# Low parts of sixteen context weights: from VectorE subtractions to accumulating transfers and ScalarE casts

## The chip, the core and the metric

The kernel runs on one core of a Trainium2 chip. The metric is the device time of one execution in microseconds; lower is better. The time before the change is the median of three runs.

## The reference

Three blocks are computed one after another on 512 tokens of width 1024: a first block (differential attention, a multi-scale pooling branch, attention over 256 memory tokens, a gated mix, a feed-forward part with a causal convolution of width 3), and two layers of a second model that has a latent stream of 512 tokens and a context stream of 256 tokens. The part that bears on the change is the layer called even, whose input weight (`in_ev_w` on the device) and output weight (`in_ev_o`) are used for the context as well as for the latent tokens:

```python
def project(h):
    aq, ak, av, ag, bq, bk, bv, bg = split_cols(h @ w_in, EVEN_WIDTHS)
    aq = rms_norm_2(heads(aq, A_HEADS), q_gain)
    ak = rms_norm_2(heads(ak, A_KV_HEADS), k_gain)
    ...
aq, ak, av, ag, bq, bk, bv, bg = project(h_lat)
c_aq, c_ak, c_av, c_ag, c_bq, c_bk, c_bv, c_bg = project(h_ctx)
...
y_ctx = jnp.concatenate([oa_c * jax.nn.silu(c_ag), ob_c * jax.nn.silu(c_bg)], axis=-1) @ w_out
```

All inputs are float32. The first block's two residual sums, `x + rms_norm(mix @ w_out)` and `x + rms_norm(ff)`, are what runs at the two boundaries named below.

## The kernel before

Activations lie feature-major: a tile has 128 features on the partitions and 512 tokens (256 for the context) along the free axis, eight tiles for 1024 features. A weight is taken in pieces of 1024 x 128 (512 KB), and one piece gives one **product**: 128 output features for all tokens, summed over eight blocks of 128 inputs. Every large product is split in three terms. A float32 operand is divided in a high part, which is the value rounded to TensorE's own format fp32r (`whi` for a weight, `hh` for an activation), and a low part, the rest (`wlo`, `hl`); `mm3` issues high x high, high x low and low x high into the same PSUM tile, so a product is 24 matmuls. All of them are recorded at the helper `mm`, L286.

Preparing a piece of weight takes three steps, in the class `Product` (L455 and on). `load` lets SP bring the piece from HBM into a buffer `raw` (L466; three buffers). `parts` lets ScalarE cast it to `whi` (L476; three buffers) and VectorE subtract, `wlo = raw - whi` (L483; two buffers). `step` issues the matmuls of one block and, after the last, the product's evacuation. A second way of making the low part is written out in `parts` and `low`, for products whose `adds` is set: it is never taken in this kernel, because the list `adding` holds False throughout.

What runs when is decided while the program is built. Products wait in `queue`, in batches. `fetch` (L334) keeps two products ahead of TensorE loaded and one of them prepared. A batch that serves as **filler** is advanced a little at a time between the steps of other work, `advance(filler, us)`, so that TensorE has products to do while VectorE and ScalarE work on something else. Each engine then runs its own list in that order, and waits at an instruction until its inputs and buffers are ready; nothing overtakes.

Two fillers matter here:

- At the **first boundary** (the profile's 591 to 641 us) the first block's mixing part ends. `post_norm` (L1490 and on) scales the eight tiles of the w_out product (`acc`, L1495), adds them to the residual (`x`, L1496) and takes their squares (ScalarE `sqa` and `ta`, L574 and L577, VectorE sum L578); the next normalisation splits `x` in `hh` (ScalarE, L522) and `hl` (VectorE, L523). The filler is the context's keys, values and queries of the even layer: eight pieces of `in_ev_w`.
- At the **second boundary** (1067 to 1115 us) the first block ends. `post_norm` does the same with the w_down product, and the even layer's latent input is normalised and modulated behind it (`mod_scale`: VectorE `ta` L1049, ScalarE `hh` L1051, VectorE `hl` L1052). The filler is the context's output projection `ctx_out`: eight pieces of `in_ev_o`, each evacuated into the context's residual (`cx`, L1069) and sent to HBM.

Before each filler TensorE does the last products of w_out and w_down; behind the first come the up-projection's pieces (`in_w_up`), behind the second those of `in_ev_w` for the latent tokens. Both take the plain way. SP's queue holds, beside the loads, the copies of `x` and `cx` to HBM (`xd`, `cxd`). GpSimd's work in this kernel is the division by the softmax sums (L974, L1193) and a few small tiles.

Of the kernel before, what the change touches and what calls it, by code (L numbers as in the profile page):

```python
# [21 lines left out]
KD = 8  # L22
# [179 lines left out]
def body(nc, tc, A, out, dbg=None):  # L202
# [16 lines left out]
    wp = pool(top, "wp")  # L219
# [88 lines left out]

    queue, ahead, adding = deque(), [], [False]
    END = object()
    current = [None, 0]

# [18 lines left out]

    def fetch():  # L334

        while len(ahead) < (3 if adding[0] else 2) and queue:
            pull()
        for p in ahead[:2 if adding[0] else 1]:
            p.parts()
        if ahead:  # L340
            ahead[0].low()
# [43 lines left out]
    def lazy(weights, n, products):  # L385

        made = []

        def bind(p, i):
            if not made:  # L390
                made.extend(products())
            p.x, p.evac = made[i].x, made[i].evac

        for i, src in enumerate(weights):
            p = Product(src, None, None, n, src.shape[-1] // P)
            p.bind = lambda p=p, i=i: bind(p, i)
            yield p

    def when(ready, products):
# [51 lines left out]
    class Product:  # L451
# [8 lines left out]
        adds = False  # L460

        def load(self):
            self.adds = adding[0] and not self.same and self.keep[0] is wp
            if not self.same:
                self.raw = tl(wp, [P, 1024], "raw", NRAW)
                nc.sync.dma_start(out=self.raw[:, :self.kt * P], in_=self.src)  # L466
# [37 lines left out]
    def product(src, x, evac, n=T, kt=KD):  # L504
        return [Product(src, x, evac, n, kt)]
# [885 lines left out]

    ec = Even(hc, None, ep, kpc, vtc)
    cmix = pair(cmp_, "m", n=C)
    filler = Batch(chain(ec.keys_values(True), ec.queries(0), ec.queries(1)))

    ff = {}

# [143 lines left out]
    def ctx_out(m):  # L1541
        def evac(ps):
            residual(cx[m], 0, 1, ps, m)
            nc.sync.dma_start(out=cxd[m], in_=cx[m])
        return product(A["ev_o"][m], cmix, evac, C)

    filler = Batch(p for m in range(KD) for p in ctx_out(m))
    firsts = Batch(lazy([A["ev_w"][ct] for ct in (4, 5, 0, 1, 2, 3)], T, lambda: chain(el.queries(0), el.keys_values())))
    advance(filler, 2.5)
    ss = post_norm(y, fss.rms_now(filler), "norm_ffn_post", filler)  # L1550
# [55 lines left out]
    def lat_items(n):  # L1606
# [3 lines left out]
    filler = Batch(chain(el.queries(1), lat_gate(0), lat_gate(1), when(lambda: 3 in el.qd, el.queries(2)), lat_gate(2),  # L1610
                         when(lambda: 7 in el.qd, el.queries(3)), *(lat_gate(m) for m in range(3, 8))))
# [269 lines left out]
```

## Time and profile before

| | |
|---|---|
| median of three runs | 1740.97 us (1740.2 to 1741.71) |
| the profiled execution's own time | 1742.39 us |
| its span, first to last instruction | 1740.4 us |
| mean granted TensorE clock | 0.982 |
| TensorE, VectorE, ScalarE, GpSimd busy | 95%, 75%, 50%, 11% of the span |
| DMA | 227.06 MB, 130 GB/s mean |

All times of instructions are from the profiled execution, in microseconds from the start of its span. Busy time is the sum of the instructions' durations on an engine; idle time before a group is put down to what ended it. A chain of waits is followed backwards from an end: at each step to what released it. The granted clock is the share of full speed that the chip gave TensorE in a stretch.

### The profile page before, as it was taken

How to read it: one execution, taken by the hardware profiler on the slowest of the kernel's cores; microseconds unless marked ns; L12 is line 12 of the kernel's file. 1: busy time of each engine (PE TensorE's matmuls, PEld its weight loads, DVE VectorE, ACT ScalarE, POOL GpSimd, SP SyncE). 2: the span in 40 equal slices, each digit the busy share in tenths (PEclk: the TensorE clock that was granted, in tenths of full speed). 3: DMA queues.
4: the chain of work that ended last, by engine and by line, in shares of the span. 5: the costliest groups of instructions: out<-in, count | busy, mean ns of one | idle time of the engine just before them, and what ended most of it. 6: DMA issues, size and time to landing. Idle time of an engine off the chain costs nothing.

```text
span 1740.4 us, 24824 instructions
## 1 busy us (share of the span) xinstructions
PE 1659.9 (95%) x8712; PEld 1392.3 (80%) x8712; DVE 1303.5 (75%) x2605; ACT 876.6 (50%) x1628; POOL 191.3 (11%) x261
## 2 busy tenths in 40 slices
PE   8999999999999989999999999899999999999897
PEld 6878878888787878888887778777888787888677
DVE  7967776777599587755775687678887665999984
ACT  6542225555333446654774343346677544554462
POOL 0120000000000000001000000002233101233200
PEclk9999999999899989999999999999999899999999
DMA  5345556445175343433332554442222446444131
GB/s 198 121 140 181 182 179 161 121 111 144 65 254 182 123 139 98 127 100 127 108 109 85 195 183 159 153 121 74 61 74 73 134 140 187 130 119 115 62 122 59
DMA packets 84875, 227.06 MB, mean 130 GB/s; under 512 B 12048, under 2 KB 24720, under 8 KB 84752
## 3 DMA queue, kind: packets, MB, share of 16 engines
q1 hardware_dynamic: 81728, 219.46, 40.5%
q10 hardware_dynamic: 3024, 6.03, 1.0%
q8 instruction: 69, 1.13, 0.3%
q14 instruction: 54, 0.44, 0.1%
HBM read 181.93 MB, written 9.44 MB: 110 GB/s over the span
## 4 chain that ended last, share of the span: by engine, by line
PE 75%; DVE 16%; ACT 3%; DMA 3%; issue 2%; POOL 0%; SPq 0%; DVEq 0%; ACTq 0%; POOLq 0%
PE mm L286 62%; PE tr L286 6%; PE s L286 3%; DVE mixf L1789 3%; PE tr L612 3%; DVE wlo L483 2%; DVE ptl L519 2%; ACT sb L1188 1%; DVE sb L1183 1%; DVE mj L863 1%; DMA cb<-in_cond 1%; DVE x L1496 1%; DVE hl L519 1%; ACT whi L476 0%; DVE acc L1495 0%
## 5 line engine op out<-in xcount | busy, mean ns | idle before, releaser
L286 PE MATMUL mm<-hh,whi 128*128 128x512 f32 (+1 forms) x1472 | 583.9, 397 | 18.2 <-ACT whi L476 7.0
L286 PE MATMUL mm<-hh,wlo 128*128 128x512 f32 (+1 forms) x1472 | 564.2, 383 | 8.9 <-DVE wlo L483 8.9
L286 PE MATMUL mm<-hl,whi 128*128 128x512 f32 (+1 forms) x1472 | 563.5, 383 | 2.0 <-DVE hl L1052 1.9
L476 ACT CAST whi<-raw 128x1024 fp32r<-128x1024 f32 (+2 forms) x264 | 268.6, 1018 | 336.1 <-PE mm L286 257.4
L483 DVE TENSOR_TENSOR wlo<-raw,whi 128x1024 fp32r<-128x1024 f32 (+2 forms) x264 | 311.7, 1181 | 85.5 <-PE mm L286 68.8
L286 PEld LDWEIGHTS mm<-hh,wlo 128*128 128x128 f32 x1472 | 281.5, 191 | 68.8 <-DVE wlo L483 12.5
L286 PEld LDWEIGHTS mm<-hh,whi 128*128 128x128 f32 x1472 | 282.7, 192 | 64.2 <-ACT whi L476 8.4
L286 PEld LDWEIGHTS mm<-hl,whi 128*128 128x128 f32 x1472 | 283.1, 192 | 45.8 <-DVE hl L1052 3.1
L1193 POOL TENSOR_SCALAR sb<-sb,l 128x256 f32<-128x256 f32 (+3 forms) x128 | 125.5, 981 | 919.2 <-DVE l L1192 859.1
L518 ACT CAST pth<-tr 128x512 fp32r<-128x512 f32 (+2 forms) x240 | 101.3, 435 | 91.7 <-PE tr L612 90.5
L519 DVE TENSOR_TENSOR ptl<-tr,pth 128x512 fp32r<-128x512 f32 (+2 forms) x240 | 116.0, 497 | 30.0 <-ACT pth L518 28.2
L612 PE MATMUL tr<-c,sb 128*128 128x128 f32 x624 | 106.0, 278 | 15.5 <-DVE ptl L519 10.0
L612 PEld LDWEIGHTS tr<-c,sb 128*128 128x128 f32 x624 | 78.7, 144 | 41.9 <-DVE ptl L519 10.3
L863 DVE CUSTOM_DVE_ANT_0 mj<-mraw,cb 128x1024 f32<-128x1024 f32 x88 | 107.5, 1222 | 0.7
L1789 DVE SCALAR_TENSOR_TENSOR mixf<-up,vec,mixf 128x512 f32<-128x512 f32 x120 | 92.0, 768 | 0.5
L286 PE MATMUL s<-kp,qd 128*128 128x256 f32 (+3 forms) x320 | 75.9, 334 | 0.7 <-ACT sb L1188 0.7
L1188 ACT ACTIVATE sb<-sb,mn 128x513 f32<-128x513 f32 (+3 forms) x64 | 49.8, 779 | 45.1 <-DVE mn L1183 44.8
L286 PE MATMUL mm<-ffh,whi 128*128 128x512 f32 x176 | 70.3, 400 | 1.1 <-ACT ffh L518 1.1
L286 PE MATMUL mm<-ffl,whi 128*128 128x512 f32 x176 | 69.9, 397 | 0.2 <-DVE ffl L519 0.2
L286 PE MATMUL mm<-ffh,wlo 128*128 128x512 f32 x176 | 69.7, 396 | 0.0
L968 ACT ACTIVATE sb<-sb,mn 128x128 f32<-128x128 f32 (+3 forms) x64 | 35.5, 555 | 54.7 <-DVE mn L966 45.4
L286 PE MATMUL mm<-mixh,whi 128*128 128x512 f32 (+1 forms) x168 | 58.7, 349 | 0.9 <-DVE mixf L1225 0.9
(383 smaller groups left out, 2694.0 us busy)
## 6 DMA issues: line engine op xcount, KB each, us to landing
raw<-in_w_in SPq DMA_DIRECT2D x56, 512.0 KB, 3.7
mraw<-in_mod_w SPq DMA_DIRECT2D x48, 512.0 KB, 3.9
raw<-in_w_up SPq DMA_DIRECT2D x44, 512.0 KB, 3.4
raw<-in_ev_w SPq DMA_DIRECT2D x40, 512.0 KB, 3.4
raw<-in_od_w SPq DMA_DIRECT2D x36, 512.0 KB, 3.4
qd<-hl SPq DMA_DIRECT2D x48, 256.0 KB, 5.1
raw<-in_w_d SPq DMA_DIRECT2D x16, 512.0 KB, 3.3
raw<-in_ev_o SPq DMA_DIRECT2D x16, 512.0 KB, 3.4
```

The lines of the kernel that those rows point to most:

```text
L286: on_pe(nc.tensor.matmul(ps, l, r, start=start, stop=stop), max(n * 0.00042, 0.107) * (2 if l.dtype == F32 else 1))
L476: S.copy(out=self.hi[:, :n], in_=self.raw[:, :n])
L483: V.tensor_tensor(out=self.lo[:, :n], in0=self.raw[:, :n], in1=f32(self.hi[:, :n]), op=ALU.subtract)
L518: S.copy(out=hi, in_=src)
L519: V.tensor_tensor(out=lo, in0=src, in1=f32(hi), op=ALU.subtract)
L612: on_pe(nc.tensor.transpose(out=ps[:, k * P:(k + 1) * P], in_=src(b), identity=ident), 0.107)
L863: tc.keep_in_program_order(V.tensor_tensor_reduce(out=jk, in0=raw, in1=cb[:, n, :], scale=0.5, scalar=0.0, op0=ALU.mult, op1=ALU.add, accu ...
L968: S.activation(out=sb[:, c, :n], in_=sb[:, c, :n], func=AF.Exp, scale=-1.0, bias=mn[:, c:c + 1], accum_out=l[:, c:c + 1])
L1183: V.tensor_tensor_reduce(out=sb, in0=src, in1=bt, scale=1.0, scalar=start, op0=ALU.add, op1=ALU.min, accum_out=mn)
L1188: S.activation(out=sb if bias is None else src, in_=src, func=AF.Exp, scale=-1.0, bias=mn, accum_out=l[:, 0:1])
L1193: G.tensor_scalar(out=sb, in0=sb, scalar1=l[:, 0:1], scalar2=0.0, op0=ALU.mult, op1=ALU.add)
L1789: V.scalar_tensor_tensor(out=u[m], in0=up[:, j:j + T], scalar=wc(j), in1=u[m], op0=ALU.mult, op1=ALU.add)
```

## The change

The flag list `adding` goes. A new generator `added` marks the products that it passes on, and it is put around the two fillers named above, so that sixteen pieces, eight at each boundary, take the second way. While any of the products ahead is marked, `fetch` loads three ahead instead of two and prepares two instead of one.

```diff
-    queue, ahead, adding = deque(), [], [False]
+    queue, ahead = deque(), []
...
-        while len(ahead) < (3 if adding[0] else 2) and queue:
+        while len(ahead) < 2 + any(p.adds for p in ahead) and queue:
             pull()
-        for p in ahead[:2 if adding[0] else 1]:
+        for p in ahead[:1 + any(p.adds for p in ahead)]:
             p.parts()
...
+    def added(products):
+
+        for p in products:
+            p.adds = True
+            yield p
+
...
         def load(self):
-            self.adds = adding[0] and not self.same and self.keep[0] is wp
...
-    filler = Batch(chain(ec.keys_values(True), ec.queries(0), ec.queries(1)))
+    filler = Batch(added(chain(ec.keys_values(True), ec.queries(0), ec.queries(1))))
...
-    filler = Batch(p for m in range(KD) for p in ctx_out(m))
+    filler = Batch(added(p for m in range(KD) for p in ctx_out(m)))
```

The second way, which stands in the code of both kernels, with `S` ScalarE and `G` GpSimd:

```python
def parts(self):
    ...
        S.copy(out=self.hi[:, :n], in_=self.raw[:, :n])
        if self.adds:
            G.tensor_scalar(out=self.raw[:, :n], in0=f32(self.hi[:, :n]), scalar1=-1.0, scalar2=0.0, op0=ALU.mult, op1=ALU.add)
            G.dma_start(out=self.raw[:, :n], in_=self.src, accum_op=ALU.add)
    ...
def low(self):
    if self.adds and self.lo is None:
        ...
        self.lo = tl(wp, [P, 1024], "wlo", NW, F32R)
        S.copy(out=self.lo[:, :n], in_=self.raw[:, :n])
```

GpSimd overwrites the raw buffer with the negated high part, a transfer then adds the same piece of weight from HBM to it, and ScalarE casts the sum to `wlo`, in front of the product that uses it. The buffers stay as many as they were. In the changed file the lines behind the new function stand 5 or 6 lower: `whi` L481, the negation L484, the transfer L485, the new cast L494, `ta` L582, `sqa` and `sqb` L579, `hh` L527 and L1056, `acc` L1500, `x` L1501, `hl` L528, `tg` L1106.

ScalarE at the second boundary, before, from the second of the filler's pieces (a number behind a name is the buffer's; `acc_5907` and `x_9734` are the first block's tiles):

```order
L476 CAST whi_9766<-raw_9758 128x1024
L577 ACTIVATE ta_9704<-acc_5907 128x512
L476 CAST whi_9816<-raw_9764 128x1024
L577 ACTIVATE ta_9727<-acc_5907 128x512
L476 CAST whi_9849<-raw_9814 128x1024
L476 CAST whi_9895<-raw_9847 128x1024
L476 CAST whi_9943<-raw_9893 128x1024
L574 ACTIVATE sqa_9884<-x_9734 128x512
```

and the same place with the change:

```order
L481 CAST whi_9782<-raw_9774 128x1024
L582 ACTIVATE ta_9720<-acc_5923 128x512
L494 CAST wlo_9786<-raw_9772 128x1024
L481 CAST whi_9790<-raw_9776 128x1024
L582 ACTIVATE ta_9743<-acc_5923 128x512
L494 CAST wlo_9794<-raw_9774 128x1024
L481 CAST whi_9842<-raw_9788 128x1024
L494 CAST wlo_9846<-raw_9776 128x1024
L481 CAST whi_9877<-raw_9840 128x1024
L494 CAST wlo_9881<-raw_9788 128x1024
L579 ACTIVATE sqa_9914<-x_9750 128x512
```

Each low part's cast stands behind the high part's cast of the piece after it: `raw_9774` is cast high in the first row and low in the sixth, and `raw_9776` is cast high between.

The end of the second filler on ScalarE, with the change (`whi_10061` belongs to the first piece behind the filler, `wlo_10065` to the filler's last):

```order
L481 CAST whi_10061<-raw_10018 128x1024
L582 ACTIVATE ta_10030<-x_9750 128x512
L582 ACTIVATE ta_10033<-x_9750 128x512
L1567 DMA rope_10140<-in_rope 128x1024
L1570 DMA bmask_10151<-in_bmask 128x1152
L494 CAST wlo_10065<-raw_9973 128x1024
L481 CAST whi_10217<-raw_10059 128x1024
L481 CAST whi_10252<-raw_10215 128x1024
L1056 ACTIVATE hh_10138<-ta_10163,mres_76 128x512
```

The last low part's cast stands behind the high part of the first plain piece and ahead of two more high parts and the eight `hh`; before, the same rows stood here without it, since VectorE made that low part.

VectorE at the first boundary, before (from `wlo_5561`, the low part of the filler's fourth piece):

```order
L483 TENSOR_TENSOR wlo_5561<-raw_5519,whi_5559 128x1024
L1495 SCALAR_TENSOR_TENSOR acc_5119<-acc_5119,vec_69,tr_5567 128x512 x2
L1496 TENSOR_TENSOR x_5239<-x_5239,acc_5119 128x512
L1090 TENSOR_TENSOR vtc_4588<-mm_5579,vtc_4588 128x2x2x64
L1496 TENSOR_TENSOR x_5239<-x_5239,acc_5119 128x512
L523 SCALAR_TENSOR_TENSOR hl_5468<-x_5239,vec_69,hh_5467 128x512
L1495 SCALAR_TENSOR_TENSOR acc_5119<-acc_5119,vec_69,tr_5567 128x512
L523 SCALAR_TENSOR_TENSOR hl_5468<-x_5239,vec_69,hh_5467 128x512
L1496 TENSOR_TENSOR x_5239<-x_5239,acc_5119 128x512
L483 TENSOR_TENSOR wlo_5620<-raw_5557,whi_5618 128x1024
```

and with the change:

```order
L1500 SCALAR_TENSOR_TENSOR acc_5119<-acc_5119,vec_69,tr_5581 128x512 x2
L1501 TENSOR_TENSOR x_5239<-x_5239,acc_5119 128x512
L1095 TENSOR_TENSOR vtc_4588<-mm_5544,vtc_4588 128x2x2x64
L1501 TENSOR_TENSOR x_5239<-x_5239,acc_5119 128x512
L528 SCALAR_TENSOR_TENSOR hl_5476<-x_5239,vec_69,hh_5475 128x512
L1500 SCALAR_TENSOR_TENSOR acc_5119<-acc_5119,vec_69,tr_5581 128x512
L528 SCALAR_TENSOR_TENSOR hl_5476<-x_5239,vec_69,hh_5475 128x512
L1501 TENSOR_TENSOR x_5239<-x_5239,acc_5119 128x512
```

The two subtractions are gone, and the steps of `post_norm` follow each other without them. GpSimd's list, which has nothing at these places before, gains eight pairs of a negation and a transfer at each boundary, ahead of the attention's divisions. TensorE's list reads the same before and after but for tile names.

## Rows read from the trace of the kernel before

**Rows 1.** The page, busy us, share of the span and instructions of each engine.

```profile
PE 1659.9 (95%) x8712; PEld 1392.3 (80%) x8712; DVE 1303.5 (75%) x2605; ACT 876.6 (50%) x1628; POOL 191.3 (11%) x261
```

**Rows 2.** The page, chain that ended last, by engine.

```profile
PE 75%; DVE 16%; ACT 3%; DMA 3%; issue 2%; POOL 0%; SPq 0%; DVEq 0%; ACTq 0%; POOLq 0%
```

**Rows 3.** Busy us and instructions by engine, granted clock, DMA share, GB/s, in three stretches.

```profile
610.00:620.00 10.00, 5.44 (x27) 5.23 (x28) 10.00 (x16) 5.11 (x9) 0.00 (x0) 0.66 0.38 131
1090.00:1100.00 10.00, 8.17 (x65) 7.72 (x64) 8.56 (x20) 3.08 (x4) 0.00 (x0) 0.98 0.95 343
1067.00:1115.00 48.00, 38.51 (x254) 34.30 (x253) 43.45 (x77) 20.92 (x28) 0.00 (x0) 0.93 0.55 192
```

**Rows 4.** Chain of waits, 597 to 633 us: shares by line; pieces (start, us, what).

```profile
by line: DVE wlo L483 17.9%; DVE x L1496 13.8%; PE mm L286 13.8%; DVE hl L523 13.8%; DVE acc L1495 11.5%; DVE sqa L578 10.7%; issue 7.8%; PE tr L286 5.2%; DVE vtc L1090 0.9%; DVE ta L542 0.8%; DVE sqb L578 0.6%; DVE rs_t L561 0.5%; DVE rs_t
...
597.40 1.23 DVE wlo L483
...
621.22 1.02 DVE wlo L483
...
624.10 1.14 DVE wlo L483
```

**Rows 5.** Chain of waits, 1068 to 1115 us: shares by line; pieces (start, us, what).

```profile
by line: PE mm L286 22.2%; DVE wlo L483 13.3%; DVE ta L1049 11.4%; DVE x L1496 10.4%; DVE hl L1052 10.1%; DVE acc L1495 8.8%; DVE sqa L578 6.7%; PE tr L286 5.8%; issue 5.5%; DVE cx L1069 3.8%; DVE rs_y L559 0.4%; DVE rs_y L562 0.4%; DVE rs_
...
1074.04 0.88 DVE wlo L483
...
1097.33 1.13 DVE wlo L483
...
1110.74 0.83 DVE wlo L483
```

**Rows 6.** TensorE's waits, 591 to 641, then 1067 to 1115: total us, times, longest.

```profile
PE mm L286 <- DVE wlo L483: 5.4, 2, 4.4
...
PE mm L286 <- DVE wlo L483: 3.8, 3, 2.4
```

**Rows 7.** The page, costliest groups, VectorE's low parts: busy us, mean ns, idle before.

```profile
L483 DVE TENSOR_TENSOR wlo<-raw,whi 128x1024 fp32r<-128x1024 f32 (+2 forms) x264 | 311.7, 1181 | 85.5 <-PE mm L286 68.8
```

**Rows 8.** ScalarE's groups of instructions, 597 to 627 us: busy us, mean ns, idle before.

```profile
L476 ACT CAST whi<-raw 128x1024 fp32r<-128x1024 f32 x6 | 6.3, 1047 | 2.7 <-PE mm L286 2.6
L522 ACT ACTIVATE hh<-x,vec 128x512 fp32r<-128x512 f32 x8 | 5.7, 719 | 5.1 <-DVE x L1496 5.1
L577 ACT ACTIVATE ta<-x 128x512 f32<-128x512 f32 x7 | 4.3, 617 | 0.0
```

**Rows 9.** GpSimd's groups over the whole span, two shapes of one line.

```profile
L974 POOL TENSOR_SCALAR sb<-sb,l 128x512 f32<-128x512 f32 x8 | 5.6, 698 | 53.7 <-PE mm L286 49.6 <-DVE l L972 4.1
...
L974 POOL TENSOR_SCALAR sb<-sb,l 128x128 f32<-128x128 f32 x8 | 3.0, 374 | 164.6 <-DVE l L972 142.5 <-PE tr L286 22.1
```

**Rows 10.** DMA issues over the span: times, KB each, median us to landing.

```profile
raw<-in_ev_o SPq DMA_DIRECT2D x16, 512.0 KB, 3.4
...
cb<-in_cond ACTq DMA_DIRECT2D x6, 512.0 KB, 7.8
```

**Rows 11.** ScalarE's timeline, an instruction of each boundary: start, us, line, what.

```profile
591.72 0.60 ACT L577 ACTIVATE ta<-mm 128x512 f32<-128x512 f32 x1
...
1069.85 1.04 ACT L476 CAST whi<-raw 128x1024 fp32r<-128x1024 f32 x1 [1.38 <-PE mm L286]
```

**Rows 12.** Timeline of VectorE and GpSimd, 1503.5 to 1506 us.

```profile
1503.96 0.73 DVE L1789 SCALAR_TENSOR_TENSOR mixf<-up,vec,mixf 128x512 f32<-128x512 f32 x1
...
1504.21 1.15 POOL L1193 TENSOR_SCALAR sb<-sb,l 128x640 f32<-128x640 f32 x1 [4.70 <-DVE l L1192]
...
1504.95 0.96 DVE L1789 SCALAR_TENSOR_TENSOR mixf<-up,vec,mixf 128x512 f32<-128x512 f32 x1
```

**Rows 13.** VectorE's timeline, the low part of the second filler's last piece.

```profile
1094.45 1.21 DVE L483 TENSOR_TENSOR wlo<-raw,whi 128x1024 fp32r<-128x1024 f32 x1
```

## Prediction

> **What bounds the kernel now.** I read the engine shares first, then the chain that ended last, then the two stretches in which the edited weights are prepared, and there only the rows of the engines that the change loads or relieves. Shares of the whole span show TensorE busy 95% and VectorE 75% [rows 1], and the chain that ended last is 75% TensorE and 16% VectorE [rows 2]. So TensorE is the bound nearly everywhere, and a VectorE instruction is worth something only where VectorE leads. The two boundaries are such places. From 610 to 620 us VectorE is busy 10.00 of 10 us and TensorE 5.44, at a granted clock of 0.66; the second boundary, 1067 to 1115, has VectorE busy 43.45 of 48 and GpSimd not at all [rows 3]. In the chain of the first boundary the low parts (wlo, L483), the first at 597.40, take 17.9% of 36 us, 6.44 us; one of them, at 624.10, belongs to the feed-forward weight behind and stays, so **5.3 us** of the chain are removed [rows 4]. In the second, from 1074.04 on, they take 13.3% of 47 us, 6.25 us; the pieces at 1097.33 and 1110.74 (1.13 and 0.83) belong to the next stage's weights, so **4.3 us** go [rows 5]. TensorE's own waits for these low parts are 5.4 and 3.8 us [rows 6]. Together 9.6 us is the most that the relief can bring; the other low parts of the sixteen lie beside w_out and w_down products, where VectorE doesn't lead, and count nothing.
>
> **The change part by part.** The order lists show the same TensorE rows before and after, so no product is moved. Sixteen VectorE subtractions of 1.18 us mean [rows 7] go. In their place each weight takes four steps, one after another: on ScalarE, on GpSimd, a transfer, and on ScalarE again.
>
> The high part is cast as before: 1.05 us on ScalarE [rows 8]. GpSimd then negates it into the raw buffer. No row has 1024 columns; 128 columns take 374 ns and 512 take 698 [rows 9], 0.84 ns a column, so I estimate 698 + 512 x 0.84 = 1.13 us. GpSimd has nothing else at either boundary (0.00 busy in all three stretches of [rows 3]), and its attention rows come after them in its order, so nothing waits behind these. Then the accumulating transfer, 512 KB: no row of the kernel shows one. Its lower bound is a plain load of the same size, 3.4 us, its upper the slowest median of a 512 KB load, 7.8 us [rows 10]. I take **L = 5.6 us**, the middle: it moves the bytes of the plain load, but must also read what it adds to and is issued by another engine, and the load row is the nearer in shape, the slow row the nearer in being beside other traffic. Last, ScalarE casts the sum to the low part, as wide as the high part's cast, 1.05 us.
>
> This makes a loop. In ScalarE's order the high part of weight k+1 stands just ahead of the low part of weight k, so two weights are on their way at once, and each pair takes 1.05 + 1.13 + L + 1.05 = 3.23 + L. **One weight takes (3.23 + L)/2**: 3.3, 4.4 or 5.5 us for L of 3.4, 5.6 or 7.8. The three raw buffers make a second loop: a buffer is loaded again only after the low part's cast (VectorE's subtraction freed it before), 3.4 + 1.05 + 1.13 + L + 1.05 for three weights, 4.1 us each at L = 5.6, so it isn't the binding one. In SP's queue the x and context spills and the next stage's first loads stand behind these loads; they have that slack.
>
> First boundary. ScalarE's last square of the w_out product ends at 591.72 + 0.60 = 592.32 [rows 11]; behind it come one low cast and the high cast of the fourth weight, which ends at 594.42. Its low part is ready at 594.42 + 1.13 + L + 1.05 = 596.60 + L, and four weights later, at 4 x (3.23 + L)/2 = 6.46 + 2L, the last: 603.06 + 3L. With L = 5.6 that is 619.9; now the last one ends at 621.22 + 1.02 = 622.2 [rows 4]. So the loop lets 2.4 of the 5.3 us through. ScalarE has in that time nine casts (9.4 us), hh (5.7), squares (4.3) [rows 8] and some 2 us of evacuations: 21.4 us from 594.42 is 615.8, so it fits, but hh and squares now stand behind casts that wait, VectorE's hl and square sums wait for them, and I put 1.0 us for that. Five negations lie beside VectorE's chain. A mixf row that began while GpSimd was running took 0.96 us, its neighbour 0.73 [rows 12], 0.23 each, 1.2 us. The last low part takes its buffer after the next stage's first weight, whose subtraction now stands ahead of it, so its cast waits for a product to free one: 1.05 us. First boundary: -2.4 + 1.0 + 1.2 + 1.05 = +0.9.
>
> Second boundary. The fourth high part is cast from 1069.85 for 1.04 us [rows 11], after the same w_down products as now. The same sum gives 1070.89 + 2.18 + L + 6.46 + 2L = 1079.53 + 3L: 1096.3 at L = 5.6, where the last low part now ends at 1094.45 + 1.21 = 1095.7 [rows 13]. No relief, then, but +0.6. Four negations beside the chain: +0.9. The last low part's buffer: +1.05. And its cast stands ahead of two high parts and the eight hh of the next modulation, on which VectorE's hl and TensorE wait in turn: +1.05. Second boundary: +3.6.
>
> **Sum: +4.5 us.** The profiled execution took 1742.39 us with a span of 1740.4; with the change it would take 1746.9. It stands 1.42 above the median of the runs, 1740.97, so against that I say **1745.5 us**.
>
> The Trainium skill speaks against the small price of the negations: "SBUF — State Buffer", section Who interferes with whom, says that a VectorE instruction with two SBUF inputs shares a port with GpSimd's reads and that the second to issue is fully blocked until the first ends. The row shows 0.23 us where the two ran together for 0.41 [rows 12], so the trace agrees that there is a wait, not that it is a whole instruction; by the rule the sum would be that of the blocked port in the second rival below. The Trainium skill, "DMA: Bandwidth & Descriptors", section Anatomy of one DMA, fits a transfer issued by GpSimd as 2.0 us plus the bytes over 436 GB/s, an estimated 3.2 us for 512 KB; no run here shows such a transfer, and by that figure the sum would be that of the first rival below.
>
> **The rivals.** *Faster: the transfer lands like a plain load.* With L = 3.4 the loops end at 613.3 and 1089.7, both ahead of VectorE, and the whole 9.6 us counts; nine negations give back 2.1 and the two last buffers 2.1: -5.4, 1735.6 us. For it: the load rows are steady at 3.4, and DMA has room on the mean (0.55 of the second boundary; sixteen more transfers are 8.4 MB, half of it there, on 9.2 MB, so 0.80). Against it: from 1090 to 1100 DMA is already at 0.95 [rows 3], and a wait on a longer path replaces a 1.2 us instruction. Chance 0.20.
>
> *No difference: relief and price cancel.* At L = 4.5 the loops end at 616.6 and 1093.0: -5.3 and -2.7, with +1.0, 2.1 and 3.15 of prices, -1.8: 1739.2 us. The same comes from a port that is blocked for a whole negation: then nine cost 1.13 each, 10.2 us, and take back all 9.6 even at L = 3.4; with 2.1 for the last buffers +2.7, 1743.7 us. For it the row that shows a wait, against it that wait's size [rows 12]. Chance 0.27.
>
> *Far slower: the transfer lands like the slow load.* At L = 7.8 the loops end at 626.5 and 1102.9, 4.3 and 7.2 us after now; with the prices above (1.0 + 2.1 + 3.15) that is +17.8, 1758.8 us. It decides from about L = 6.5, beyond which each further us costs 6, three at each boundary. For it: the row of 7.8, the full DMA from 1090 on, and that the loads of the next weights share it. Longer waits of TensorE also cost clock: in the stretch where its busy time falls to 5.44 of 10 us, 0.66 was granted on the mean, between its two levels of 1.2 and 2.4 GHz [rows 3]; I add nothing for that here. Chance 0.18.
>
> That the change doesn't do what it says is excluded: the order lists show the sixteen negations, transfers and casts, and the sixteen subtractions gone.
>
> **How the numbers follow.** L from 5.5 to 6.5 is the forecast: +4 to +10, chance 0.35, and it is the likeliest of the four. About 0.2%, 3.5 us, is what a measurement of this kernel can tell from no change. Slower by more than that is the forecast and the far slower case, 0.53; within it 0.27; faster 0.20. The likeliest case's own range is 1745 to 1751; the whole range, 1735 to 1761, leaves out about half of the fastest case and half of the slowest.
>
> **What would show it.** The first thing to read is the accumulating transfer's own time to landing: 5 to 6.5 us bears out L, under 4 the first rival, over 7 the last. Each low cast on ScalarE should be preceded by idle time that ends with that transfer, one to two us at a time, and the pace from one low cast to the next should be 4 to 5 us. VectorE should have idle time at both boundaries where it now has none, waiting for ScalarE's hh and squares. VectorE's instructions that begin beside a negation should be 0.2 to 0.3 us longer; over 0.8 would mean the blocked port. The end of the first boundary should come within 3 us of now, that of the second 2 to 5 us later. I am wrong if the second boundary ends earlier, if TensorE's waits there shrink, or if the transfers take under 4 us.

## The result: 1.25% slower

The changed kernel takes 1762.4 us (median of four runs, 1760.8 to 1766.36) against 1741.34 for the kernel before on the same chips. The ratio is 1.0125, 95% interval 1.0107 to 1.0144: 18.6 to 25.1 us more. The forecast was 1745.5 with a range of 1735 to 1761; the direction was right, the size was not, and the time lies just above the range, next to the rival that was called far slower (1758.8). In what follows a ratio is turned into microseconds with 1741.

The profile of the changed kernel has a span of 1760.2. Its page, engines, DMA queues and chain (the row of the engines answers to [rows 1], the chain to [rows 2]):

```profile
PE 1665.0 (95%) x8712; PEld 1396.8 (79%) x8712; DVE 1292.0 (73%) x2589; ACT 890.7 (51%) x1644; POOL 221.7 (13%) x293
...
q1 hardware_dynamic: 81728, 219.46, 40.6%
q0 software_dynamic: 2304, 8.39, 2.7%
...
PE 73%; DVE 14%; DMA 5%; ACT 4%; issue 2%; POOL 1%; SPq 0%; ACTq 0%; DVEq 0%; POOLq 0%
```

VectorE's busy time fell by 11.5 us, ScalarE's rose by 14 and GpSimd's by 30: the work did move. But 5% of the chain that ended last is now DMA, where 3% was, and TensorE's busy time did not fall. The sixteen adding transfers have a queue of their own, q0, of 8.39 MB. The views by boundary say where that DMA stands. The chain of waits, from 587 to 640 us and then from 1066 to 1134 us:

```profile
by line: DMA raw<-in_ev_w 37.9%; PE mm L286 21.1%; issue 8.7%; POOL raw L484 6.1%; ACT whi L481 5.8%; PE tr L286 3.5%; ACT wlo L494 2.8%; ACT hh L527 2.5%; DVE sqa L583 2.3%; ACT ta L582 2.0%; DVE hl L528 1.5%; DVE x L1501 1.3%; ACT tg L110
...
594.06 6.40 DMA raw<-in_ev_w
...
604.02 7.66 DMA raw<-in_ev_w
...
617.28 6.03 DMA raw<-in_ev_w
...
by line: DMA raw<-in_ev_o 39.3%; PE mm L286 15.8%; issue 7.9%; POOL raw L484 7.1%; DVE hl L1057 7.0%; DVE ta L1054 6.8%; ACT wlo L494 6.0%; ACT whi L481 4.6%; PE tr L286 2.5%; DVE cx L1074 1.4%; DVE wlo L488 1.2%; ACT ta L582 1.1%; ACTq L49
...
1076.13 6.02 DMA raw<-in_ev_o
...
1085.79 6.98 DMA raw<-in_ev_o
...
1097.09 8.32 DMA raw<-in_ev_o
```

In [rows 4, 5] VectorE led both stretches and no transfer was on the chain. Now the adding transfers alone take 37.9% of 53 us, 20.1 us, and 39.3% of 68 us, 26.7 us. Their time from issue to landing, beside that of the copies of x and of the context that share the DMA engines:

```profile
xd<-x SPq DMA_DIRECT2D x24, 256.0 KB, 4.9
...
raw<-in_ev_w POOLq DMA_DIRECT2D x8, 512.0 KB, 5.9
...
raw<-in_ev_o POOLq DMA_DIRECT2D x8, 512.0 KB, 6.6
...
cxd<-cx SPq DMA_DIRECT2D x8, 128.0 KB, 5.8
```

The plain load of the same piece lands in 3.4 us [rows 10]; the adding one takes 5.9 and 6.6 us at the median. The loop that the prediction drew is in the trace. ScalarE's timeline at the second boundary, the fifth and the seventh piece's low parts with what lies between, and the last low part:

```profile
1092.87 1.04 ACT L494 CAST wlo<-raw 128x1024 fp32r<-128x1024 f32 x1 [3.13 <-DMA raw<-in_ev_o]
1093.82 0.63 ACT L582 ACTIVATE ta<-x 128x512 f32<-128x512 f32 x1
1094.35 1.04 ACT L481 CAST whi<-raw 128x1024 fp32r<-128x1024 f32 x1
...
1105.51 1.04 ACT L494 CAST wlo<-raw 128x1024 fp32r<-128x1024 f32 x1 [4.56 <-DMA raw<-in_ev_o]
...
1114.69 1.04 ACT L494 CAST wlo<-raw 128x1024 fp32r<-128x1024 f32 x1 [5.56 <-PE mm L286]
```

and GpSimd's, for the seventh piece:

```profile
1095.49 1.20 POOL L484 TENSOR_SCALAR raw<-whi 128x1024 f32<-128x1024 f32 x1 [3.85 <-ACT whi L481]
1097.09 0.89 POOL L485 DMA_DIRECT2D raw<-in_ev_o  x1 [0.41 <-POOL raw L484]
```

A low part is cast at 1092.87; behind it come a square and the high part of the seventh piece (1094.35), its negation (1095.49), a gap of 0.41, the transfer's issue at 1097.09, its landing 8.3 us later, and only then the low part at 1105.51. That is 12.6 us for two weights. Who waits for whom, from 1066 to 1134: ScalarE, VectorE, TensorE (total us, times, longest):

```profile
ACT wlo L494 <- DMA raw<-in_ev_o: 20.1, 7, 4.6
...
ACT wlo L494 <- PE mm L286: 5.6, 1, 5.6
...
DVE sqa L583 <- ACT ta L582: 11.1, 6, 3.9
...
PE mm L286 <- ACT wlo L494: 10.5, 6, 3.2
PE mm L286 <- DVE cx L1074: 5.1, 1, 5.1
```

ScalarE stands 20.1 us for landings. VectorE stands 11.1 for squares (ta) that are queued behind the waiting casts (in the trace of before these sums at this boundary waited for none), and TensorE waits for low parts, and 5.1 us in one piece for a context evacuation (cx), which stands in VectorE's list behind such a sum. Busy time by stretch (the columns of [rows 3]):

```profile
606.00:616.00 10.00, 5.85 (x37) 5.65 (x37) 6.33 (x11) 6.56 (x12) 2.14 (x3) 0.75 1.01 266
616.00:626.00 10.00, 7.65 (x47) 6.89 (x47) 9.60 (x16) 8.57 (x16) 3.96 (x4) 0.84 0.86 213
1085.00:1095.00 10.00, 6.47 (x52) 6.06 (x52) 7.48 (x12) 5.29 (x7) 3.20 (x4) 1.00 1.00 263
1095.00:1105.00 10.00, 6.29 (x40) 5.88 (x38) 6.09 (x10) 3.43 (x5) 4.18 (x4) 0.83 1.04 302
```

VectorE has idle time in all of these stretches now (it is busy 6.33 of 10 us from 606 to 616, where [rows 3] has 10.00 from 610 to 620). TensorE is worse off at the second boundary: busy 6.47 and 6.29 of 10 us, where [rows 3] has 38.51 of 48. The DMA share is 0.86 to 1.04.

### The profile page after: what moved, and what is told of

It reads as the page before. It is cut to its first block, busy times and chain, and to the rows that moved or that the text cites. A ratio compares the mean times of both kernels' runs of the same rounds, so it can differ in the third digit from the quotient of the medians.

```text
span 1760.2 us, 24891 instructions
## 1 busy us (share of the span) xinstructions
PE 1665.0 (95%) x8712; PEld 1396.8 (79%) x8712; DVE 1292.0 (73%) x2589; ACT 890.7 (51%) x1644; POOL 221.7 (13%) x293
## 3 DMA queue, kind: packets, MB, share of 16 engines
q1 hardware_dynamic: 81728, 219.46, 40.6%
q0 software_dynamic: 2304, 8.39, 2.7%
q10 hardware_dynamic: 3024, 6.03, 1.0%
q8 instruction: 69, 1.13, 0.3%
## 4 chain that ended last, share of the span: by engine, by line
PE 73%; DVE 14%; DMA 5%; ACT 4%; issue 2%; POOL 1%; SPq 0%; ACTq 0%; DVEq 0%; POOLq 0%
PE mm L286 61%; PE tr L286 6%; PE s L286 4%; DVE mixf L1794 3%; PE tr L617 3%; DVE wlo L488 2%; DVE ptl L524 2%; DMA raw<-in_ev_o 2%; DMA raw<-in_ev_w 1%; ACT whi L481 1%; ACT sb L1193 1%; DVE sb L1188 1%; DVE mj L868 1%; DVE hl L524 1%; DMA cb<-in_cond 1%
## 5 line engine op out<-in xcount | busy, mean ns | idle before, releaser
L481 ACT CAST whi<-raw 128x1024 fp32r<-128x1024 f32 (+2 forms) x264 | 268.5, 1017 | 321.0 <-PE mm L286 258.7
L488 DVE TENSOR_TENSOR wlo<-raw,whi 128x1024 fp32r<-128x1024 f32 (+1 forms) x248 | 292.3, 1179 | 84.6 <-PE mm L286 66.6
L617 PE MATMUL tr<-c,sb 128*128 128x128 f32 x624 | 105.3, 277 | 15.5 <-DVE ptl L524 10.1
```

Of the source, the lines that this page charges most:

```text
L481: S.copy(out=self.hi[:, :n], in_=self.raw[:, :n])
L488: V.tensor_tensor(out=self.lo[:, :n], in0=self.raw[:, :n], in1=f32(self.hi[:, :n]), op=ALU.subtract)
L617: on_pe(nc.tensor.transpose(out=ps[:, k * P:(k + 1) * P], in_=src(b), identity=ident), 0.107)
```

## Experiments

Each run has as its ratio the comparison with the kernel before on the same chip. The first four divide the change.

**First boundary alone.**

```diff
-    filler = Batch(added(p for m in range(KD) for p in ctx_out(m)))
+    filler = Batch(p for m in range(KD) for p in ctx_out(m))
```

> Only the first filler's eight pieces take the second way; the second filler is as before. Theory A (the traces of before and after: from the last w_out evacuation to the second filler's first high part the change costs 4.3 us, behind it 14.3): 4 to 6 us over the kernel before, about 1746. Theory B (the sum of the prediction, the two boundaries nearly alike once the transfer's real landing of 6.0 to 6.4 us is put in): 8 to 10 us over.

1747.28 us, ratio 1.0037 (1.0018 to 1.0055): +6.4 us.

**Second boundary alone.**

```diff
-    filler = Batch(added(chain(ec.keys_values(True), ec.queries(0), ec.queries(1))))
+    filler = Batch(chain(ec.keys_values(True), ec.queries(0), ec.queries(1)))
```

> Only the second filler's eight pieces take the second way. Theory A: 13 to 16 us over the kernel before, about 1755, most of what the whole change costs. Theory B: 8 to 11 us over. If the two parts' costs do not add up to some 20 us, one boundary's lateness is partly taken back by the other's or by what lies between, against both.

1758.17 us, 1.0096 (1.0066 to 1.0127): +16.7 us. The two add up to 23.1, the whole to 21.8. Theory A holds, though both lie a little above its ranges (4 to 6 and 13 to 16): the boundaries are not alike, and the second costs over twice as much. The prediction's sums were +0.9 and +3.6. No sign that anything is taken back in between.

**No transfer.**

```diff
-                    G.dma_start(out=self.raw[:, :n], in_=self.src, accum_op=ALU.add)
```

> The accumulating transfer is left out and ScalarE casts the negated high part as the low part (so the low parts of the sixteen weights do not hold the rest); the negation and both casts stay. Theory A (the transfer and what waits behind it is the whole price): the loop is 3.2 us for two weights, VectorE's relief of up to 9.6 us shows, less the negations' waits: 1731 to 1739. Rival C (ScalarE's sixteen added casts, the negations on the shared port and the changed order are a large part of the price whatever the transfer takes): 1743 to 1752.

1741.43 us, 0.9998 (0.9984 to 1.0011). Neither: without the transfer the price is gone, so the transfer and what waits for it are the price, but the relief doesn't appear. ScalarE stood 7.0 us at the second boundary before the last low part, for a buffer; that suggested the next pair of runs.

**A copying transfer on the same queue.**

```diff
-                    G.dma_start(out=self.raw[:, :n], in_=self.src, accum_op=ALU.add)
+                    G.dma_start(out=self.raw[:, :n], in_=self.src)
```

> The transfer stays on GpSimd's queue with the same 512 KB, but copies in place of adding (so the sixteen low parts hold the whole weight, not the rest). Theory D (the adding itself is slow: in the trace the queue's transfers kept the sixteen DMA engines busy 2.97 us each, a plain load of this size 1.71): time to landing falls from 6.0 to under 4.8 us and the whole to 1744 to 1752. Rival E (GpSimd's queue is slow, whatever the transfer does): landing stays at 5.5 us or more, and the time within 3 us of the changed kernel's 1762.

1757.43 us, 1.0089 (1.0057 to 1.012): +15.5. Its DMA queue and landings:

```profile
q0 software_dynamic: 2304, 8.39, 1.5%
...
raw<-in_ev_w POOLq DMA_DIRECT2D x8, 512.0 KB, 4.3
...
raw<-in_ev_o POOLq DMA_DIRECT2D x8, 512.0 KB, 5.0
```

Theory D was right on the transfer and not on the time. The adding does cost DMA time: q0 takes 1.5% of the sixteen engines' span, 26.4 us for sixteen transfers, 1.65 us each; in the changed kernel 2.7%, 47.5 us, 2.97 each (q1, which holds the plain loads with all other sizes, comes to 1.71 for 512 KB: 40.6% for 219.46 MB). The shares are rounded, so each figure is good to some 0.05. Landing falls to 4.3 and 5.0 us. But only some 6 us of 22 come back.

**The order of low buffers.** In the changed kernel the plain piece behind a filler takes its low buffer early, the filler's last piece late.

```diff
-        for p in ahead[:1 + any(p.adds for p in ahead)]:
+        for n, p in enumerate(ahead[:1 + any(p.adds for p in ahead)]):
+            if n and not p.adds:
+                break
             p.parts()
```

> The changed kernel, but a plain product behind a marked one takes its low buffer only after the marked one has its own (in the changed kernel the last low part of each filler waits until a product frees a buffer; at the second boundary ScalarE stood 5.6 us there, 7.0 where the transfer was left out). Theory F (that wait is a good part of the second boundary's 14 us): 5 to 8 us under the changed kernel's 1762, 1754 to 1757. Rival G (the wait only took the place of the transfer's own lateness, which ends a little earlier): less than 2.5 us under.

1764.17 us, 1.0139 (1.0124 to 1.0154): +24.2. Theory F falls: the wait of 5.6 us only stood in the place of others. This order was kept in most of the runs that follow.

**The same without a transfer.** The edit of the third run, on top.

> The same order of buffers, and no accumulating transfer (the low parts of the sixteen weights hold the negated high part's rounding, not the rest). Theory F: the order of buffers is what kept the run without a transfer at 1741; without it VectorE's relief shows, 1732 to 1737. Rival G: within 2 us of 1741, the relief of 9.6 us is not there to be had, because ScalarE or TensorE ends the stages anyway.

1738.18 us, 0.9988 (0.9975 to 1.0001): -2.1. Between F and G, nearer to G. Busy time at the first boundary (columns as in [rows 3]):

```profile
600.00:610.00 10.00, 6.58 (x51) 5.94 (x50) 9.87 (x15) 9.32 (x17) 2.15 (x2) 0.99 0.59 220
610.00:620.00 10.00, 7.80 (x52) 7.35 (x52) 9.39 (x16) 9.42 (x17) 1.19 (x1) 0.84 0.62 171
```

ScalarE is busy 9.3 and 9.4 of 10 us, VectorE still 9.9 and 9.4: now neither has room.

**GpSimd subtracts in one instruction.**

```diff
-                    G.tensor_scalar(out=self.raw[:, :n], in0=f32(self.hi[:, :n]), scalar1=-1.0, scalar2=0.0, op0=ALU.mult, op1=ALU.add)
-                    G.dma_start(out=self.raw[:, :n], in_=self.src, accum_op=ALU.add)
+                    self.lo = tl(wp, [P, 1024], "wlo", NW, F32R)
+                    G.tensor_tensor(out=self.lo[:, :n], in0=self.raw[:, :n], in1=f32(self.hi[:, :n]), op=ALU.subtract)
```

> The sixteen low parts are subtracted by GpSimd in one instruction, with the loads, buffers and look-ahead of the kernel before; no transfer, no cast. If GpSimd takes about twice VectorE's 1.2 us and shares its port, theory F gives 1735 to 1741, VectorE's relief less the shared port. Rival H (the shared port blocks VectorE for each whole instruction): 1745 to 1755, slower than before.

1749.51 us, 1.0057 (1.0042 to 1.0072): +9.9. Rival H. One such subtraction takes 2.4 us alone. VectorE's timeline from 602 us, and GpSimd's at the same place:

```profile
602.03 0.75 DVE L528 SCALAR_TENSOR_TENSOR hl<-x,vec,hh 128x512 fp32r<-128x512 f32 x1
...
603.35 2.25 DVE L528 SCALAR_TENSOR_TENSOR hl<-x,vec,hh 128x512 fp32r<-128x512 f32 x1
605.52 2.89 DVE L1501 TENSOR_TENSOR x<-x,acc 128x512 f32<-128x512 f32 x1
608.33 0.68 DVE L583 TENSOR_TENSOR sqa<-sqa,ta 128x512 f32<-128x512 f32 x1
```

```profile
602.09 5.77 POOL L485 TENSOR_TENSOR wlo<-raw,whi 128x1024 fp32r<-128x1024 f32 x2 [1.61 <-ACT hh L527]
```

The same `hl` takes 0.75 us and, beside GpSimd, 2.25; the sum `x` 2.89 where 0.68 is usual. VectorE is held for nearly the whole of GpSimd's instruction.

**A copying transfer with this order of buffers.** The edit of the fourth run on the fifth's kernel.

> The order of buffers of the fifth run, with a copying transfer in place of the adding one (the low parts hold the whole weight). With the fifth and sixth runs this divides the price: adding against copying, copying against nothing. Theory D (the adding is the price of the transfer): within 5 us of the run without a transfer. Rival E (any transfer in this place costs, its latency in a loop of two weights): at least 8 us above the run without, and within 6 us of the fifth run.

1757.55 us, 1.0097 (1.008 to 1.0114): +16.9, which is 19.0 above the run without a transfer and 7.3 under the fifth (the rival allowed 6). Rival E: any transfer in this place costs, the adding adds a smaller part.

**An eighth of the bytes.**

```diff
-                    G.dma_start(out=self.raw[:, :n], in_=self.src, accum_op=ALU.add)
+                    G.dma_start(out=self.raw[:, :P], in_=self.src[:, :P], accum_op=ALU.add)
```

> The fifth run's kernel, but only the first 128 of a piece's 1024 columns are added by the transfer, 64 KB instead of 512 (the other columns of the sixteen low parts don't hold the rest). Theory J (the loop of two weights: a transfer costs nothing until the loop is longer than VectorE's own pace, then some 6 us per us): it should land in 2 to 3.5 us, the loop is shorter than VectorE's pace, and the time is within 4 us of the run without a transfer, 1736 to 1742. Theory K (the price is in proportion to the landing, since every wait of ScalarE is passed on): 1746 to 1752.

1750.58 us, 1.0058 (1.0035 to 1.0081): +10.1. Its transfers land at a median of

```profile
raw<-in_ev_w POOLq DMA_DIRECT2D x8, 64.0 KB, 3.3
...
raw<-in_ev_o POOLq DMA_DIRECT2D x8, 64.0 KB, 3.5
```

so even 64 KB, with next to no load on the DMA engines, cost 12.2 us above the run without a transfer: theory K. The landings of all sixteen in the fifth run, the copying one on its kernel, and this one:

```profile
DMA to landing us min/median/max: 5.4/6.7/9.2
```

```profile
DMA to landing us min/median/max: 3.7/5.0/8.9
```

```profile
DMA to landing us min/median/max: 2.7/3.3/5.8
```

Median landing against price above the run without a transfer: 6.7 us and 26.3; 5.0 and 19.0; 3.3 and 12.2. That is 3.9, 3.8 and 3.7 us of time for each us of landing; the intervals of each price are some 4 us wide to either side, so the line is not finer than that. No free part shows down to 3.3 us; no run has a transfer that lands much sooner, so a free part below that is not excluded.

**Three weights on their way.**

```diff
-        while len(ahead) < 2 + any(p.adds for p in ahead) and queue:
+        while len(ahead) < 2 + 2 * any(p.adds for p in ahead) and queue:
...
-        for n, p in enumerate(ahead[:1 + any(p.adds for p in ahead)]):
+        for n, p in enumerate(ahead[:1 + 2 * any(p.adds for p in ahead)]):
...
+            p.spare = spare() if n % 4 == 3 else None
```

A spare piece takes its raw and high buffers from the boundary's own pool; for room one small tile of the normalisation has one buffer instead of two.

> The fifth run's kernel with three weights on their way instead of two (one spare raw and one spare high buffer in each boundary's own pool, used by every fourth piece; four loaded and three prepared). Theory J (latency in the loop): a weight takes a third of 3.6 + L, not half; 8 us or more of the fifth run's 24 come back, 1748 to 1756. Theory M (the DMA engines are full, 0.93 to 1.04 in the trace of the changed kernel, since an adding transfer keeps them 1.7 times as long as a plain one): the transfers only land later, 8 us and more, and the time stays within 4 us of 1764.

1750.44 us, 1.0069 (1.0043 to 1.0095): +12.0, half of the fifth run's 24.2. The landings are as late as there:

```profile
raw<-in_ev_w POOLq DMA_DIRECT2D x6, 512.0 KB, 6.8
...
raw<-in_ev_o POOLq DMA_DIRECT2D x6, 512.0 KB, 6.6
```

Theory J on this point, and M falls: as many bytes, as late a landing, half the price. What costs is a landing's length in a loop with too few weights in it. (The spare piece also lets a load start sooner, which was not tried by itself; but in the fifth run ScalarE's high casts stood only 1.0 us for plain loads at the second boundary, against 20.9 for adding transfers.)

**Every second piece marked.**

```diff
-        for p in products:
-            p.adds = True
+        for n, p in enumerate(products):
+            p.adds = n % 2 == 0
             yield p
```

> The fifth run's order of buffers, but only every second piece of the two fillers is marked, eight of sixteen. Both J and M: the loop has one transfer for two weights and the DMA engines half the added load: most of the price goes, 1740 to 1748. A rival N (each marked piece costs the same, 1.5 us, however many there are): 1750 to 1754.

1759.47 us, 1.0111 (1.0081 to 1.0141): +19.3. A miss for all three theories: half the transfers, nearly the whole price, 2.4 us for each. It speaks against the DMA engines' load once more. ScalarE's timeline in this run at the second boundary, from the high cast of one marked piece to that of the next:

```profile
1079.05 1.05 ACT L483 CAST whi<-raw 128x1024 fp32r<-128x1024 f32 x1 [1.97 <-DMA raw<-in_ev_o]
1084.06 1.04 ACT L496 CAST wlo<-raw 128x1024 fp32r<-128x1024 f32 x1 [3.96 <-DMA raw<-in_ev_o]
1085.01 1.04 ACT L483 CAST whi<-raw 128x1024 fp32r<-128x1024 f32 x1
```

A marked piece was cast high at 1075.50; the plain piece's high cast follows at 1079.05, the marked one's low cast at 1084.06, and right behind it, at 1085.01, the next marked piece's high cast. So only one marked piece is on its way at a time, and two weights still take one whole passage through high part, negation, transfer and low part, 9.5 us here. That this is the whole reason was not tried by itself.

**The relief by itself.** Three runs with the look-ahead of the kernel before: the subtractions left out; ScalarE's casts in their place; GpSimd's negations in their place.

```diff
-                    G.tensor_scalar(out=self.raw[:, :n], in0=f32(self.hi[:, :n]), scalar1=-1.0, scalar2=0.0, op0=ALU.mult, op1=ALU.add)
-                    G.dma_start(out=self.raw[:, :n], in_=self.src, accum_op=ALU.add)
+                    self.lo = self.hi
```

> The sixteen subtractions are left out and nothing takes their place: the high part serves as low part too (so these sixteen products lack their low part), with the loads and look-ahead of the kernel before. It measures the relief alone. If the chain's rows meant what the prediction took from them: 9 to 10 us under the kernel before, 1730 to 1732. If another engine is late right behind VectorE, as the run without a transfer (2 us under) suggests: 1735 to 1739.

1736.06 us, 0.9965 (0.9954 to 0.9976): -6.1. TensorE's waits in it, first boundary and second:

```profile
PE mm L286 <- ACT ta L581: 3.9, 2, 2.6
...
PE mm L286 <- DVE cx L1073: 3.8, 1, 3.8
```

With the low parts gone, TensorE waits at both boundaries for others: for ScalarE's squares and, in one piece, for the context's evacuation.

```diff
-                    self.lo = self.hi
+                    self.lo = tl(wp, [P, 1024], "wlo", NW, F32R)
+                    S.copy(out=self.lo[:, :n], in_=self.raw[:, :n])
```

> As the run before this one, but ScalarE casts the raw weight to the low part right behind the high part (so the low part holds the whole weight again, not the rest): sixteen more ScalarE casts of 1.05 us, no GpSimd, no transfer. If the casts take the relief back (ScalarE busy 9.3 and 9.4 of 10 us at the first boundary in the run without a transfer): 4 to 8 us above the run that leaves the subtractions out. If ScalarE has room: within 2 us of it, and the negations or the changed look-ahead took the relief.

1737.67 us, 0.9979 (0.9966 to 0.9991): -3.7, so 2.4 above the run before it, with some 3 us to either side: less than the 4 to 8 expected for a ScalarE without room, and not clear of nothing.

```diff
                     self.lo = self.hi
+                    G.tensor_scalar(out=self.raw[:, :n], in0=f32(self.hi[:, :n]), scalar1=-1.0, scalar2=0.0, op0=ALU.mult, op1=ALU.add)
```

> As the run that leaves the subtractions out, plus the sixteen negations on GpSimd (whose result nothing uses; the products lack their low part). By rows of the changed kernel VectorE's instructions beside a negation are 0.4 to 0.85 us longer, some 3.7 us at the two boundaries together: 1 to 4 us above the run that leaves the subtractions out. If the port is no matter: within 1 us.

1734.77 us, 0.996 (0.9947 to 0.9974): -7.0, against -6.1 without them: the same within their intervals. The negations cost nothing that shows.

## Why the prediction had the direction and not the size

**What bounds the kernel.** VectorE does lead both stretches, but the 9.6 us of chain [rows 4, 5] are not to be had: with the sixteen subtractions simply gone, 6.1 (4.2 to 8.0) come back. The prediction called 9.6 the most and used it whole in its first rival; that rival was off by more than a third, for a reason the chain can't show, what is late right behind.

**The negation.** 1.04 us at the median, 1.13 estimated. The shared port: in the changed kernel x at the first boundary takes 0.788 us on average instead of 0.682 and the square sums at the second 0.903 instead of 0.680, with hl some 3.7 us at both together, where 2.1 was put in. The prediction read 0.23 us as the size of the wait. VectorE, then GpSimd, in the changed kernel:

```profile
615.94 1.52 DVE L1501 TENSOR_TENSOR x<-x,acc 128x512 f32<-128x512 f32 x1
...
1075.15 1.11 DVE L583 TENSOR_TENSOR sqa<-sqa,ta 128x512 f32<-128x512 f32 x1 [1.82 <-ACT ta L582]
```

```profile
615.78 1.15 POOL L484 TENSOR_SCALAR raw<-whi 128x1024 f32<-128x1024 f32 x1 [5.08 <-ACT whi L481]
...
1074.68 1.04 POOL L484 TENSOR_SCALAR raw<-whi 128x1024 f32<-128x1024 f32 x1 [2.97 <-ACT whi L481]
```

The two VectorE rows end 0.53 and 0.54 us after the negation that they began beside, and so do the other five lengthened ones of this width, whenever they had begun: they were held until it ended. (`acc`, which reads one input from PSUM, was not lengthened beside the negation at 1084.34: 1.41 us for two that began within it.) The row of 0.96 us in [rows 12] fits: it ends 0.55 us after GpSimd's, of which only 0.41 was left when it began. The Trainium skill ("SBUF — State Buffer", Who interferes with whom) says that the second to issue is blocked until the first ends; the trace agrees, for the negations and for the subtractions with two inputs, where `hl` was held for 2.25 us. The second rival's blocked port was there, then, but the waits came to 3.7 us and not to 10.2. As a price they did not count: in the run with the negations alone the square sums at the second boundary are as long (0.929 us on average, 0.685 without negations), and its time is no longer, within some 3 us.

**L, the transfer.** Counted from the negation's end as in the prediction, 0.4 of gap and a median of 5.9 to 6.6, up to 8.3: 6.3 to 8.7 us, where 5.6 was taken. By the prediction's own sum 6.4 gives 4.5 + 0.8 x 6 = +9.3 us. So by the median this term explains a little over a quarter of the miss of 17.3. The chain that ended last runs through longer landings than the median: 6.40, 7.66 and 6.03 us at the first boundary, 6.02, 6.98 and 8.32 at the second. With their means and the gap, 7.1 and 7.5 us, the same sum gives 4.5 + 3 x 1.5 + 3 x 1.9 = +14.7, an estimate, and the term is over half of the miss. That is in part why the far slower rival, which took 7.8, came nearest.

**The loop: the step that failed.** A truer L alone does not mend the sum. The prediction set the end of the loop against the end of VectorE's work, boundary by boundary, and let a landing cost nothing up to the point where the later of the two changes sides: "So the loop lets 2.4 of the 5.3 us through", and for the second boundary "No relief, then, but +0.6". That takes the two for independent. They are not: the squares and hh on which VectorE works stand in ScalarE's list behind the casts that wait for a landing, and the context's evacuation, for which TensorE waits, in VectorE's list behind those. Each wait is handed on. The prediction named such waits, but put 1.0 us for them at the first boundary and, but for the last low part's 1.05, nothing at the second, where VectorE alone stood 11.1 us for squares. The runs show the price in proportion to the landing from 3.3 us on: 3.7 to 3.9 us per us with two weights on the way, 2.1 with three (12.0 + 2.1 above the run without a transfer, for a landing of 6.8). For landings of 3.3, 5.0 and 6.7, counted from the issue, the prediction's sum with 0.4 of gap gives -3, +3 and +13.5; measured are +10.1, +16.9 and +24.2. The run with 64 KB shows it best. ScalarE's timeline in it, the fourth and the last low part of the second boundary:

```profile
1075.31 1.05 ACT L496 CAST wlo<-raw 128x1024 fp32r<-128x1024 f32 x1
...
1094.56 1.03 ACT L496 CAST wlo<-raw 128x1024 fp32r<-128x1024 f32 x1
```

That is one low part every 4.8 us, no slower than VectorE's 5.1 in the kernel before (1074.04 to 1094.45), and the transfers of this run still cost 12.2 us. That the handing on is the whole of the difference is argued from the waits and lists; no run takes the waits apart.

**The pieces.** With the relief left to itself -6.1; +2.4 for the casts on ScalarE; some +1.6 for the changed look-ahead and order (to -2.1, not tried singly); +19.0 for a copying transfer in the loop; +7.3 for its adding; and about -2.4 between the fifth run's order of buffers and the changed kernel's, with overlapping intervals. Two of these, +1.6 and -2.4, are what was left over, so that the sum is the 21.8 measured shows nothing by itself.

**The last low part's buffer.** Foreseen at 1.05 us for each boundary, in the trace 0.7 and 5.6; with it gone the time did not fall. A wait that ends last is not a price if another ends just before it.

**DMA.** The prediction counted bytes and came to a share of 0.80 at the second boundary. By engine time, eight adding transfers of 2.97 us are 23.8 us beside 0.55 x 48 = 26.4, 50 of 48 us: full, as the shares of 0.86 to 1.04 show. That the landing of 8.3 us comes from there is a reading: copies, which keep the engines 1.65 us each, took up to 9.2 us too. The estimate of 3.2 us by the Trainium skill's fit ("DMA: Bandwidth & Descriptors", Anatomy of one DMA) lies below the copy's median of 4.4 in the fourth run and at half of the adding transfer's; here the measurement decides.

**TensorE's clock.** The prediction added nothing for it. For the same 8712 instructions TensorE is busy 1665.0 us in the changed kernel's profile and 1659.9 before, at mean granted clocks of 0.980 and 0.982, so that some 5 of the 19.8 us between the two spans may be slower matmuls. From one execution to the next this varies as much (1658.8 us in the run with the second boundary alone); how much of the price is clock stays open.

**What would show it.** Of the signs listed, the median landing (5.9 and 6.6 for 5 to 6.5) and VectorE's new idle time came as said. Idle time ends with the transfer before most low casts, but it is up to 4.6 us, where one to two were named. The pace is 5.8 us per low part at the second boundary (1076.28 to 1105.51, five steps), where 4 to 5 were named. VectorE's held instructions are 0.4 to 0.85 us longer, not 0.2 to 0.3. And the two boundaries cost 6.4 and 16.7 us, where an end within 3 us of the kernel before's and one 2 to 5 us later were named. No sign of being wrong that the prediction names appeared.

Not tried: a version in which the low casts wait on an engine that has nothing else to do, and one with four weights on their way. No version that computes the whole result beat the kernel before.

## What to carry to other kernels

Before moving an instruction from a full engine, leave it out: here that would have shown that 6 us was the whole prize, before any price. A stand-in that is quick on each engine but passes through four queues adds its latency to an in-order list, and everything behind it in that list, and behind that in the next engine's, pays in proportion, some 3.8 us here for each us of landing; count how many are on their way at once, and not only how busy each engine is. Where such a chain can't be avoided, a third weight on the way was worth more here than halving the transfers.

## What the hardware showed that was not expected

An adding transfer from HBM kept the sixteen DMA engines busy 2.97 us per 512 KB where a copying one took 1.65 and 512 KB of the plain queue 1.71. What ran beside it landed later: the 256 KB copies of x in 4.9 us at the median instead of 2.0, the 128 KB copies of the context in 5.8 instead of 1.8; beside the copying transfers they took 4.0 and 4.6, so most of this comes with a copying transfer too. A transfer issued by GpSimd started 0.3 to 0.4 us after the instruction before it and held GpSimd for 0.89 us when adding, 0.58 when copying; adding 64 KB still took 3.3 us to land, half of what 512 KB took. And a VectorE instruction with both inputs in SBUF that began beside a GpSimd instruction ended some 0.54 us after it, whenever it had begun: 0.68 us became 1.11 to 1.53 beside a negation, and 0.75 became 2.25 beside a subtraction with two inputs.
